# Seven block products instead of eight in two gate pairs and half of the output projection, and the sums of h in a tile of the large pool

## The chip, the core and the metric

The kernel runs on one core of one Trainium2 chip. The metric is the device time of one execution in microseconds (us), as the median of several runs; lower is better.

## What is computed

One layer of a transformer-like trunk over 256 tokens of width 2048, all in float32:

```python
h = rms_norm(x, norm_mix)
proj = h @ w_in                      # 2048 x 11264: q,f,i,g of branch A, q,k,v of branch B, gate logits
gate_a, gate_b = split(sigmoid(gate_logits + b_gate))
y_a = hgrn2_mixer(q_a, f_a, i_a, g_a)        # gated linear recurrence, 8 heads
y_b = chunked_relpos_attention(q_b, k_b, v_b)  # 8 heads
merged = gate_a * (y_a @ w_proj_a) + gate_b * (y_b @ w_proj_b)
x = x + merged @ w_out                        # 2048 x 2048
h = rms_norm(x, norm_ffn)
ff_gate, ff_up = split(h @ w_ffn_in)          # 2048 x 2*5632
out = x + (silu(ff_gate) * ff_up) @ w_ffn_out # 5632 x 2048
```

## The kernel before, in words

**The unit of work.** Every weight matrix is cut into blocks of 512 columns, and each block by rows into chunks (`kc`) of 512 rows, which are four k-tiles of 128. TensorE (PE) multiplies in a 32-bit format that keeps fewer bits than float32, so both operands are split into a high and a low part, and each product is a *triple* of matmuls (high*high, high*low, low*high; lines 162 to 164 and 216 to 218). The 256 tokens are two row blocks `m` of 128. A plain chunk of one block takes 4 k-tiles x 2 row blocks = 8 triples, 24 matmuls of 512 columns.

**Splitting the weights.** `load_weights` (lines 131 to 145) and `halves` (174 to 180) split what a DMA from SP's queue brought (`fetch`, 118): ScalarE (ACT) casts raw weights to the high part `whi` (141, 171), VectorE (DVE) subtracts to get the low part `wlo` (142, 172), two k-tiles at a time. `whi` and `wlo` have four such buffers each, the raw weights eight.

**Seven for eight.** `product_pair` (199 to 268) multiplies two blocks of columns at once. In a chunk whose number is in `forms`, the first two k-tiles x two row blocks x two column blocks are a 2x2x2 block product, made in seven triples instead of eight (`seven`, 223), from sums of blocks: of the weights, `weight_forms` (182) makes four DVE sums `ta`, `tb` (188, tiles of the pool `t6` with two buffers) and splits them; of the activations, `act_forms` (312) makes four sums `sf` (319, or 321 with a gain) and splits them. The other two k-tiles are plain. Seven triples go to eight PSUM banks: four `cb`, which end as results, and four `ub` (products 1, 5, 7, 6), which an epilogue adds on DVE afterwards. There are eight banks in all, four in the pool `mm`, four in `aux`. It is used for half of the blocks of the FFN's first product (`SEVEN_IN`, j = 1, 3, 5, 7, 9) in all four chunks, with the plain k-tiles first in chunk 0, and for the FFN's second product in chunks `SEVEN` = 1, 2, 3, 5, 6, 7, 9.

**Side work.** Generators in `running` (105) emit transposes, attention and recurrence between the triples, one step per `tick()`, every four triples. After FFN block j, `transpose_split` (301) transposes `hn` on PE, splits it into `hT` and, for j in `SEVEN`, makes the sums of h (line 307), which are stored to DRAM (`spill`, 309, a DMA from POOL's queue) and come back later. Those sums are written to a tile of the pool `t6`:

```python
        if j in SEVEN:
            f = t6_p.tile([P, 2, 4, P], F32R, tag="t6", name=nm("sform"))
            spill = kept[j] = dram.tile([P, 2, 4, P], F32, tag=f"kept{j}", name=nm("kept"))
        soon = dict(wait=0, pool=mm) if j + 1 in SEVEN_IN else {}
        start(transpose_split(hn, *hT[j], forms=f, spill=spill, **soon))
```

**The stages in order of time.** Branch A and B projections with recurrence and attention; eight gate products (lines 741 to 753: per nb the blocks of gates a and b); the merge (758 to 768: two half-length products per nb, products with the gates on DVE, their sum on POOL, line 766, then transposes to `mT`); the output projection (775 to 786); the FFN's first product (822 to 839); its second (847 to 877).

**What sets the order.** A planner orders each engine's instructions when the program is built, by priority and by a simulated time, and gives out the buffers of a pool as they come free in that simulation. Weight loading and splitting stand under a priority raised by `PREP_AHEAD` = 500 instructions. Program order of the side work is therefore only a hint; each engine then runs its list in order. The pool `t4` has 33 buffers of 4 KB per partition and holds the activations; `t2` has three of 2 KB.

Of the kernel before, what the change touches and what calls it, by code (L numbers as in the profile page):

```python
# [11 lines left out]
F32R = mybir.dt.float32r  # L12
U32 = mybir.dt.uint32
AF = mybir.ActivationFunctionType
ALU = mybir.AluOpType
AX = mybir.AxisListType

P = 128
T = 256
# [3 lines left out]
NJ = DFF // 512  # L23
# [6 lines left out]
C_NM, C_NF, C_LB, C_OG, C_QG, C_KG = 0, 16, 32, 48, 56, 57  # L30
# [5 lines left out]

SEVEN = (1, 2, 3, 5, 6, 7, 9)

SEVEN_IN = (1, 3, 5, 7, 9)


@with_exitstack
def block_kernel(ctx: ExitStack, tc: tile.TileContext, x, x_t, w_in, w_pa, w_pb, w_out, w_fi, w_fo,
                 params, b_gate, bias, masks, out):
    nc = tc.nc
# [6 lines left out]
    t6_p = ctx.enter_context(tc.tile_pool(name="t6", bufs=2))  # L52
    t2_p = ctx.enter_context(tc.tile_pool(name="t2", bufs=3))
    mm = ctx.enter_context(tc.tile_pool(name="mm", bufs=4, space=bass.MemoryType.PSUM))
    aux = ctx.enter_context(tc.tile_pool(name="aux", bufs=4, space=bass.MemoryType.PSUM))
# [4 lines left out]
    def nm(s):  # L60
        uid[0] += 1
        return f"{s}_{uid[0]}"

    def t4(shape, s, dt=F32):
        return big.tile(shape, dt, tag="t4", name=nm(s))
# [4 lines left out]
    def t2(shape, s):  # L70
        return t2_p.tile(shape, F32, tag="t2", name=nm(s))
# [19 lines left out]
    for _ in range(N_WARM):  # L91
        nc.tensor.matmul(warm_ps[:, 0:256], lhsT=warm[:, 0:P], rhs=warm, start=True,
                         stop=True)

    def rsqrt_mean(dst, ss, n):

# [15 lines left out]
    def start(g):  # L112
        running.append(g)
# [187 lines left out]
    def transpose_split(nat, hi, lo, gain=None, wait=2, pool=aux, forms=None, spill=None):  # L301
        for _ in range(wait):
            yield 1
        for pair in range(2):
            pt = transpose_split_pair(nat, pair, hi, lo, gain, pool)
            if forms is not None and pair == 0:
                act_forms(pt, forms, gain)
                if spill is not None:
                    nc.gpsimd.dma_start(out=spill, in_=forms.bitcast(F32))
            yield 1  # L310
# [30 lines left out]
    par = cpool.tile([P, NPAR], F32, tag="par", name="par")  # L341
    xs = []
    xT = []
    ss_x = cpool.tile([P, 2, 4], F32, tag="ss_x", name="ss_x")
    r1 = cpool.tile([P, 2], F32, tag="r1", name="r1")
# [6 lines left out]
    def rstd_rows(ss, r):  # L352
        tot = t_small([P, 8], "tot")
        nc.vector.tensor_reduce(out=tot[:, 0:2], in_=ss, axis=AX.X, op=ALU.add)
        rsqrt_mean(r, tot[:, 0:2], D)
# [31 lines left out]
    act_x = picker(xT)  # L387
# [335 lines left out]
    for half in range(2):  # L723
        ps = ps_f0 if half == 0 else product(w_in, 2 + half, 4, act_x)
        b, kk, qT = (t4([P, 4, T], s) for s in ("b", "kk", "qT"))
# [12 lines left out]
        start(after(1, attention(half, 0, qT, kT, v, *ybT[half])))  # L738
        start(after(4, attention(half, 1, qT, kT, v, *ybT[half])))

    gates = {}
    for nb in range(4):
        for br in range(2):
            c = 4 * br + nb
            bg = t2([P, 512], "bg")
            nc.sync.dma_start(out=bg, in_=b_gate[c:c + 1, :].to_broadcast([P, 512]))
            ps = product(w_in, 14 + c, 4, act_x)
            gt = t4([P, 2, 512], "gate")
            for m in range(2):
                nc.vector.scalar_tensor_tensor(out=gt[:, m, :], in0=ps[m], scalar=r1[:, m:m + 1],  # L750
                                               in1=bg, op0=ALU.mult, op1=ALU.add)
                nc.scalar.activation(gt[:, m, :], gt[:, m, :], AF.Sigmoid)
            gates[br, nb] = gt


    act_a, act_b = picker(yaT), picker(ybT)
    mT = []
    for nb in range(4):
        ga, gb = gates[0, nb], gates[1, nb]
        ps = product(w_pa, nb, 2, act_a)  # L760
        for m in range(2):
            nc.vector.tensor_tensor(out=ga[:, m, :], in0=ps[m], in1=ga[:, m, :], op=ALU.mult)
        ps = product(w_pb, nb, 2, act_b)
        for m in range(2):
            nc.vector.tensor_tensor(out=gb[:, m, :], in0=ps[m], in1=gb[:, m, :], op=ALU.mult)
            nc.gpsimd.tensor_tensor(out=gb[:, m, :], in0=ga[:, m, :], in1=gb[:, m, :], op=ALU.add)
        mT.append(split_tiles("mT"))
        start(transpose_split(gb, *mT[nb]))


    act_m = picker(mT)
    x2T, x2_kept, fx = [], [], {}
    ss2 = cpool.tile([P, 2, 4], F32, tag="ss2", name="ss2")
    r2 = cpool.tile([P, 2], F32, tag="r2", name="r2")
    for nb in range(4):
        ps = product(w_out, nb, 4, act_m)
        for m in range(2):
            nc.vector.tensor_tensor(out=xs[nb][:, m, :], in0=ps[m], in1=xs[nb][:, m, :],
                                    op=ALU.add)
        x2T.append(split_tiles("x2T"))  # L780
        fx[nb] = t4([P, 2, 4, P], "fx", F32R)
        start(transpose_split(xs[nb], *x2T[nb], gain=par[:, C_NF + 4 * nb:C_NF + 4 * nb + 4],
                              forms=fx[nb]))
        sumsq_block(xs[nb], ss2, nb)
        x2_kept.append(dram.tile([P, 2, 512], F32, tag=f"x2_{nb}", name=nm("x2")))
        nc.gpsimd.dma_start(out=x2_kept[nb], in_=xs[nb])
    rstd_rows(ss2, r2)


    act_x2 = picker(x2T)  # L790
    hT = []
    kept = {}
    def add(out, a, b):
        nc.vector.tensor_tensor(out=out, in0=a, in1=b, op=ALU.add)

    def up_times(hn, m, up):
        nc.vector.scalar_tensor_tensor(out=hn[:, m, :], in0=up, scalar=r2[:, m:m + 1],
                                       in1=hn[:, m, :], op0=ALU.mult, op1=ALU.mult)
# [1 line left out]
    def swiglu_pair(j):  # L800
        hn = t4([P, 2, 512], "hn")
        u = []

        def sums(ub):
            u.extend(t2([P, 512], "u") for _ in range(2))
            nc.scalar.copy(hn[:, 0, :], ub[1])
            add(u[0], ub[6], hn[:, 0, :])
            add(hn[:, 1, :], ub[7], u[0])
            add(u[1], ub[5], hn[:, 1, :])
            add(u[0], ub[5], u[0])  # L810

        cb = product_pair(w_fi, (j, NJ + j), 4, act_x2, fx, aux, mm, sums, plain_first=True,
                          last=True)
        for m in range(2):
            add(hn[:, m, :], cb[m, 0], hn[:, m, :])
            nc.scalar.activation(hn[:, m, :], hn[:, m, :], AF.Silu, scale=r2[:, m:m + 1])
        for m in range(2):
            add(u[m], cb[m, 1], u[m])
            up_times(hn, m, u[m])
        return hn  # L820

    for j in range(NJ):
        if j in SEVEN_IN:
            hn = swiglu_pair(j)
        else:
            ps = product(w_fi, j, 4, act_x2)
            hn = t4([P, 2, 512], "hn")
            for m in range(2):
                nc.scalar.activation(hn[:, m, :], ps[m], AF.Silu, scale=r2[:, m:m + 1])
            ps = product(w_fi, NJ + j, 4, act_x2)  # L830
            for m in range(2):
                up_times(hn, m, ps[m])
        hT.append(split_tiles("hT"))
        f = spill = None
        if j in SEVEN:
            f = t6_p.tile([P, 2, 4, P], F32R, tag="t6", name=nm("sform"))
            spill = kept[j] = dram.tile([P, 2, 4, P], F32, tag=f"kept{j}", name=nm("kept"))
        soon = dict(wait=0, pool=mm) if j + 1 in SEVEN_IN else {}
        start(transpose_split(hn, *hT[j], forms=f, spill=spill, **soon))

    act_h = picker(hT)
    out_v = out.rearrange("(m p) d -> p m d", p=P)
    forms = {}
# [3 lines left out]
    for pair in range(2):  # L847
        nbs = (2 * pair, 2 * pair + 1)
        xs = {nb: t4([P, 2, 512], "x2") for nb in nbs}
        for nb in nbs:  # L850
            nc.gpsimd.dma_start(out=xs[nb], in_=x2_kept[nb])
        x0, x1 = (xs[nb] for nb in nbs)

        def sums(ub):

            u2, u3 = t2([P, 512], "u2"), t2([P, 512], "u3")
            add(x0[:, 0, :], x0[:, 0, :], ub[1])
            nc.scalar.copy(u2, ub[1])
            add(u2, ub[6], u2)
            add(u3, ub[7], u2)  # L860
            add(x1[:, 0, :], x1[:, 0, :], u2)
            add(x0[:, 1, :], x0[:, 1, :], u3)
            add(x1[:, 1, :], x1[:, 1, :], u3)
            for m in range(2):
                add(x1[:, m, :], ub[5], x1[:, m, :])

        pools = (mm, aux) if pair == 0 else (aux, mm)
        cb = product_pair(w_fo, nbs, NJ, act_h, forms, *pools, sums, last=pair == 1)
        for n, nb in enumerate(nbs):
            for m in range(2):  # L870
                pieces = 2 if nb == 3 and m == 1 else 1
                w = 512 // pieces
                for i in range(pieces):
                    sl = slice(i * w, (i + 1) * w)
                    add(xs[nb][:, m, sl], cb[m, n][:, sl], xs[nb][:, m, sl])
                    nc.sync.dma_start(out=out_v[:, m, nb * 512 + i * w:nb * 512 + (i + 1) * w],
                                      in_=xs[nb][:, m, sl])
# [63 lines left out]
```

## Time and profile before

| what | us |
|---|---|
| median of 3 runs | 1447.47 (1447.43 to 1447.57) |
| the profiled execution, its own time | 1449.29 |
| its span, first to last instruction | 1447.5 |
| PE busy | 1431.1 (99%) |
| VectorE busy | 990.4 (68%) |
| ScalarE busy | 749.2 (52%) |
| GpSimd busy | 48.5 (3%) |

The mean granted clock of TensorE is 0.995 of full speed, and the DMA queues moved 287 MB. A matmul's row shows the start and a modelled end; matmuls overlap, so the distance of their starts is what one costs, not its duration. Some matmul rows are missing from the trace. Idle time stands in brackets at the end of a row, with what ended it.

### The profile page before, as it was taken

The numbers are of one execution on the slowest core, as the hardware profiler recorded it, in microseconds if no ns is written. First come the engines' busy times: TensorE is split into PE (matmuls) and PEld (weight loads), VectorE is DVE, ScalarE is ACT, GpSimd is POOL, SyncE is SP. The second block draws the span as 40 slices with busy tenths as digits, with TensorE's granted clock in tenths as the row PEclk, the third lists the DMA queues.
The fourth block names the chain that finished last, engine by engine and source line by source line (L and its number), as shares of the span: only waits on it lengthen the run. The fifth ranks groups of instructions, "written<-read, shape, count | busy, mean of one in ns | idle before, by whom it ended". The sixth has DMA issues, their size and how long they took to land.

```text
span 1447.5 us, 17485 instructions
## 1 busy us (share of the span) xinstructions
PE 1431.1 (99%) x6484; PEld 1185.8 (82%) x6484; DVE 990.4 (68%) x1225; ACT 749.2 (52%) x966; POOL 48.5 (3%) x59
## 2 busy tenths in 40 slices
PE   8999999999999999999999999999999999999998
PEld 7888888888888888888888877888778888888887
DVE  6768869564654555556658768687686876777876
ACT  6756655555544444445555535455354554454553
POOL 0100100100000000100000000000000001000000
PEclk9999999999999999999999999999999999999999
DMA  9654454456556665556655646656466578666662
GB/s 356 235 196 154 137 198 148 168 172 207 181 198 203 203 192 191 189 183 218 204 194 177 227 150 213 208 178 228 147 216 207 178 236 314 230 200 224 203 190 85
DMA packets 81526, 287.32 MB, mean 198 GB/s; under 512 B 9120, under 2 KB 9376, under 8 KB 81440
## 3 DMA queue, kind: packets, MB, share of 16 engines
q1 hardware_dynamic: 78272, 274.66, 57.1%
q0 software_dynamic: 3168, 11.54, 2.1%
q8 instruction: 51, 0.84, 0.2%
q14 instruction: 35, 0.29, 0.1%
HBM read 278.30 MB, written 7.86 MB: 198 GB/s over the span
## 4 chain that ended last, share of the span: by engine, by line
PE 88%; issue 9%; DMA 1%; DVE 1%; ACT 0%; SPq 0%; POOL 0%; DVEq 0%; ACTq 0%; POOLq 0%
PE mm L162 19%; PE mm L164 19%; PE mm L163 19%; PE mp L216 9%; PE mp L217 9%; PE mp L218 9%; PE bank L279 2%; PE bank L537 1%; DMA xt<-in_x_t 1%; DMA kept<-sform 0%; PE bank L567 0%; PE bank L613 0%; PE bank L664 0%; ACT whi L171 0%; DVE tb L188 0%
## 5 line engine op out<-in xcount | busy, mean ns | idle before, releaser
L142 DVE TENSOR_TENSOR wlo<-raw,whi 128x1024 fp32r<-128x1024 f32 (+1 forms) x340 | 411.5, 1215 | 283.8 <-ACT whi L141 283.4
L141 ACT CAST whi<-raw 128x1024 fp32r<-128x1024 f32 (+1 forms) x340 | 352.9, 1042 | 384.6 <-PE mm L164 332.1
L162 PE MATMUL mm<-whi,xTh 128*128 128x512 f32 x704 | 276.9, 397 | 2.5 <-ACT whi L141 2.5
L164 PE MATMUL mm<-whi,xTl 128*128 128x512 f32 x704 | 274.9, 390 | 0.0
L163 PE MATMUL mm<-wlo,xTh 128*128 128x512 f32 x704 | 274.8, 390 | 0.0
L172 DVE TENSOR_TENSOR wlo<-raw,whi 128x1024 fp32r<-128x1024 f32 (+1 forms) x168 | 183.2, 1112 | 37.9 <-ACT whi L171 37.2
L171 ACT CAST whi<-raw 128x1024 fp32r<-128x1024 f32 (+1 forms) x168 | 157.0, 965 | 98.8 <-PE mp L218 53.6
L162 PEld LDWEIGHTS mm<-whi,xTh 128*128 128x128 f32 x704 | 132.1, 188 | 29.4 <-ACT whi L141 3.6
L164 PEld LDWEIGHTS mm<-whi,xTl 128*128 128x128 f32 x704 | 132.2, 188 | 27.6
L163 PEld LDWEIGHTS mm<-wlo,xTh 128*128 128x128 f32 x704 | 132.3, 188 | 26.9 <-DVE wlo L142 0.9
L162 PE MATMUL mm<-whi,x2Th 128*128 128x512 f32 x384 | 150.0, 391 | 0.0
L164 PE MATMUL mm<-whi,x2Tl 128*128 128x512 f32 x384 | 149.5, 389 | 0.0
L163 PE MATMUL mm<-wlo,x2Th 128*128 128x512 f32 x384 | 149.4, 389 | 0.0
L217 PE MATMUL mp<-wlo,hTh 128*128 128x512 f32 x282 | 109.7, 389 | 0.0
L218 PE MATMUL mp<-whi,hTl 128*128 128x512 f32 x282 | 109.6, 389 | 0.0
L216 PE MATMUL mp<-whi,hTh 128*128 128x512 f32 x282 | 99.7, 390 | 0.0
L218 PE MATMUL mp<-whi,x2Tl 128*128 128x512 f32 x220 | 87.5, 398 | 0.0
L217 PE MATMUL mp<-wlo,x2Th 128*128 128x512 f32 x220 | 87.4, 397 | 0.0
L164 PEld LDWEIGHTS mm<-whi,x2Tl 128*128 128x128 f32 x384 | 72.1, 188 | 15.0
L163 PEld LDWEIGHTS mm<-wlo,x2Th 128*128 128x128 f32 x384 | 72.1, 188 | 14.8
L162 PEld LDWEIGHTS mm<-whi,x2Th 128*128 128x128 f32 x384 | 72.1, 188 | 14.8
L216 PE MATMUL mp<-whi,x2Th 128*128 128x512 f32 x220 | 79.7, 405 | 0.0
(221 smaller groups left out, 1898.5 us busy)
## 6 DMA issues: line engine op xcount, KB each, us to landing
raw<-in_w_fi SPq DMA_DIRECT2D x176, 512.0 KB, 4.6
raw<-in_w_in SPq DMA_DIRECT2D x172, 512.0 KB, 4.4
raw<-in_w_fo SPq DMA_DIRECT2D x88, 512.0 KB, 5.0
raw<-in_w_out SPq DMA_DIRECT2D x32, 512.0 KB, 3.6
raw<-in_w_pa SPq DMA_DIRECT2D x16, 512.0 KB, 4.5
raw<-in_w_pb SPq DMA_DIRECT2D x16, 512.0 KB, 4.6
x<-x POOLq DMA_DIRECT2D x8, 512.0 KB, 4.6
kept<-sform POOLq DMA_DIRECT2D x7, 512.0 KB, 4.6
```

The costliest lines, as they stand in the source:

```text
L141: nc.scalar.copy(hi[:, sl, :], src[:, sl, :])
L142: nc.vector.tensor_tensor(out=lo[:, sl, :], in0=src[:, sl, :], in1=hi[:, sl, :].bitcast(F32), op=ALU.subtract)
L162: nc.tensor.matmul(ps[m], lhsT=ah, rhs=wh, start=kc == 0 and k4 == 0, stop=False)
L163: nc.tensor.matmul(ps[m], lhsT=ah, rhs=wl, start=False, stop=False)
L164: nc.tensor.matmul(ps[m], lhsT=al, rhs=wh, start=False, stop=kc == n_chunks - 1 and k4 == 3)
L171: nc.scalar.copy(hi, src)
L172: nc.vector.tensor_tensor(out=lo, in0=src, in1=hi.bitcast(F32), op=ALU.subtract)
L216: nc.tensor.matmul(ps, lhsT=ah, rhs=wh, start=first, stop=False)
L217: nc.tensor.matmul(ps, lhsT=ah, rhs=wl, start=False, stop=False)
L218: nc.tensor.matmul(ps, lhsT=al, rhs=wh, start=False, stop=final)
L279: nc.tensor.transpose(out=pt[:, j, m * P:(m + 1) * P], in_=nat[:, m, c:c + P], identity=ident)
L537: nc.tensor.matmul(pl[:, j, :], lhsT=ek[:, g // 2, (g % 2) * P:(g % 2 + 1) * P], rhs=eq[:, g, :], start=True, stop=True)
```

## The change

Three things, and helpers that move:

- The gates of nb = 1 and nb = 3 (`SEVEN_GATE`): the blocks of gate a and gate b become one `product_pair` with sums in all four chunks, `cb` in `aux` and `ub` in `mm`. The sums of x that it needs (`fq`) are made by a new generator `x_forms`, started ahead of the gates: it loads two of four k-tiles of each chunk of x transposed once more (POOL's queue), and makes the sums with the gain.
- The output projection's column blocks 0 and 1 (`SEVEN_OUT`) become one `product_pair`. The sums of the merged activations (`fm`) are made in the transposes of the merge; those of nb = 3 come one tick earlier than before and in the pool `mm`. Residual add, transposes and sums of squares of both blocks follow together.
- The sums of h (`sform`) are written to a `t4` tile instead of a `t6` tile.

```diff
+SEVEN_GATE = (1, 3)
+SEVEN_OUT = (0,)
...
-    gates = {}
+    def four_sums(ub, e00, e10, e01, e11):
+        nc.scalar.copy(e00, ub[1])
+        add(e01, ub[6], e00)
+        add(e10, ub[7], e01)
+        add(e11, ub[5], e10)
+        add(e01, ub[5], e01)
+
+    def x_forms():
+        for c in range(4):
+            xt = t4([P, 2, T], "xt2")
+            nc.gpsimd.dma_start(out=xt, in_=x_t[c, :, 0:2, :])
+            fq[c] = t4([P, 2, 4, P], "fq", F32R)
+            yield 1
+            yield 1
+            act_forms(xt, fq[c], par[:, C_NM + 4 * c:C_NM + 4 * c + 4])
+
+    gates, fq = {}, {}
+    start(x_forms())
     for nb in range(4):
+        bgs, gts = [], []
         for br in range(2):
             c = 4 * br + nb
...
+            if nb in SEVEN_GATE:
+                continue
             ps = product(w_in, 14 + c, 4, act_x)
...
+        if nb in SEVEN_GATE:
+            def sums(ub):
+                for br in range(2):
+                    gates[br, nb] = t4([P, 2, 512], "gate")
+                four_sums(ub, *(gates[br, nb][:, m, :] for br in range(2) for m in range(2)))
+
+            cb = product_pair(w_in, (14 + nb, 18 + nb), 4, act_x, fq, aux, mm, sums,
+                              plain_first=True, last=True)
+            for br in range(2):
+                gt = gates[br, nb]
+                for m in range(2):
+                    add(gt[:, m, :], cb[m, br], gt[:, m, :])
+                    nc.vector.scalar_tensor_tensor(out=gt[:, m, :], in0=gt[:, m, :],
+                                                   scalar=r1[:, m:m + 1], in1=bgs[br],
+                                                   op0=ALU.mult, op1=ALU.add)
+                    nc.scalar.activation(gt[:, m, :], gt[:, m, :], AF.Sigmoid)
...
-        start(transpose_split(gb, *mT[nb]))
+        fm[nb] = t4([P, 2, 4, P], "fm", F32R)
+        soon = dict(wait=1, pool=mm) if nb == 3 else {}
+        start(transpose_split(gb, *mT[nb], forms=fm[nb], **soon))
...
+    def residual_sums(x0, x1):      # the second FFN product's epilogue, moved here
+        ...
+    for pair in range(2):
+        nbs = (2 * pair, 2 * pair + 1)
+        if pair in SEVEN_OUT:
+            cb = product_pair(w_out, nbs, 4, act_m, fm, aux, mm,
+                              residual_sums(xs[nbs[0]], xs[nbs[1]]), plain_first=True, last=True)
+            for n, nb in enumerate(nbs):
+                norm_block(nb, [cb[m, n] for m in range(2)])
+        else:
+            for nb in nbs:
+                norm_block(nb, product(w_out, nb, 4, act_m))
...
-            f = t6_p.tile([P, 2, 4, P], F32R, tag="t6", name=nm("sform"))
+            f = t4([P, 2, 4, P], "sform", F32R)
```

`norm_block` is the body of the old loop over the output blocks (residual add, transposes, sum of squares, store of x). `residual_sums` has one ACT copy and eight DVE adds.

## Rows read from the trace of the kernel before

**Rows 1.** The page: busy time of each engine; the chain that ended last.

```profile
PE 1431.1 (99%) x6484; PEld 1185.8 (82%) x6484; DVE 990.4 (68%) x1225; ACT 749.2 (52%) x966; POOL 48.5 (3%) x59
...
PE 88%; issue 9%; DMA 1%; DVE 1%; ACT 0%; SPq 0%; POOL 0%; DVEq 0%; ACTq 0%; POOLq 0%
```

**Rows 2.** Who PE waited for: us in total, times, longest.

```profile
PE mp L216 <- ACT whi L171: 7.8, 4, 3.0
...
PE mp L217 <- DVE wlo L172: 1.1, 2, 0.5
```

**Rows 3.** PE in order of time in a plain gate product: start, duration, line.

```profile
437.65 0.39 PE L163 MATMUL mm<-wlo,xTh 128*128 128x512 f32 x1
...
446.49 0.39 PE L163 MATMUL mm<-wlo,xTh 128*128 128x512 f32 x1
```

**Rows 4.** Stretches: length, PE, PEld, DVE, ACT, POOL busy (count), granted clock, DMA, GB/s.

```profile
819.85:914.14 94.29, 89.94 (x391) 73.12 (x390) 68.03 (x83) 46.05 (x54) 1.11 (x2) 0.96 0.58 190
...
914.14:1000.41 86.27, 86.27 (x391) 71.33 (x390) 66.19 (x78) 45.45 (x52) 0.53 (x1) 1.00 0.60 201
...
1000.41:1094.89 94.48, 90.02 (x392) 73.23 (x390) 68.03 (x83) 46.08 (x54) 1.07 (x2) 0.96 0.56 190
...
1094.89:1181.15 86.26, 86.26 (x392) 71.34 (x389) 66.12 (x78) 45.47 (x52) 0.53 (x1) 1.00 0.60 201
...
870.00:880.00 10.00, 9.13 (x27) 7.10 (x28) 7.59 (x10) 5.33 (x6) 0.00 (x0) 0.66 0.75 245
```

**Rows 5.** PE in order of time, j = 3, where it idled.

```profile
865.54 0.73 PE L216 MATMUL mp<-whi,fx 128*128 128x512 f32 x2 [0.96 <-ACT whi L171]
...
866.80 0.50 PE L217 MATMUL mp<-wlo,fx 128*128 128x512 f32 x1 [0.53 <-DVE wlo L172]
...
870.87 0.79 PE L216 MATMUL mp<-whi,fx 128*128 128x512 f32 x1 [2.86 <-ACT whi L171]
```

**Rows 6.** DVE in order of time at the start of j = 3.

```profile
860.42 0.28 DVE L319 TENSOR_TENSOR sf<-bank,sf 128x128 f32<-128x128 f32 x1
...
863.08 0.68 DVE L188 TENSOR_TENSOR ta<-raw,raw 128x512 f32<-128x512 f32 x1
...
868.24 0.69 DVE L188 TENSOR_TENSOR tb<-ta,raw 128x512 f32<-128x512 f32 x1 [1.49 <-DMA kept<-sform]
```

**Rows 7.** DVE, then PE, in order of time at j = 1.

```profile
778.34 1.23 DVE L172 TENSOR_TENSOR wlo<-tb,whi 128x1024 fp32r<-128x1024 f32 x1
...
780.18 0.39 PE L217 MATMUL mp<-wlo,fx 128*128 128x512 f32 x1
```

**Rows 8.** Groups by line and shape: total us, mean ns of one | idle before.

```profile
L319 DVE TENSOR_TENSOR sf<-bank,sf 128x128 f32<-128x128 f32 x28 | 7.6, 286 | 0.4
...
L172 DVE TENSOR_TENSOR sform<-sf,sform 128x512 fp32r<-128x512 f32 x7 | 4.8, 685 | 0.0
...
L321 DVE SCALAR_TENSOR_TENSOR sf<-bank,par,sf 128x128 f32<-128x128 f32 x16 | 5.2, 344 | 0.1
...
L188 DVE TENSOR_TENSOR ta<-raw,raw 128x512 f32<-128x512 f32 x34 | 23.4, 690 | 15.2 <-DMA raw<-in_w_fi 9.1 <-DMA raw<-in_w_fo 5.6
...
L172 DVE TENSOR_TENSOR wlo<-ta,whi 128x1024 fp32r<-128x1024 f32 x34 | 41.6, 1224 | 45.7 <-ACT whi L171 45.7
...
L794 DVE TENSOR_TENSOR u<-mp,u 128x512 f32<-128x512 f32 x19 | 12.5, 678 | 0.0
```

**Rows 9.** The same view: two gate products, the merge, two output products.

```profile
391.00:434.50 43.50, 43.50 (x200) 36.25 (x199) 21.62 (x20) 20.55 (x24) 0.00 (x0) 1.00 0.60 195
...
547.00:637.50 90.50, 90.50 (x412) 74.85 (x411) 54.41 (x55) 36.63 (x38) 14.14 (x8) 1.00 0.57 189
...
683.20:728.70 45.50, 45.50 (x210) 37.61 (x209) 29.12 (x40) 24.44 (x36) 1.79 (x3) 1.00 0.62 208
```

**Rows 10.** POOL and DVE in order of time at the merge's end.

```profile
629.98 3.54 POOL L766 TENSOR_TENSOR gate<-gate,gate 128x512 f32<-128x512 f32 x2 [19.22 <-DVE gate L765]
...
630.73 1.63 DVE L142 TENSOR_TENSOR wlo<-raw,whi 128x1024 fp32r<-128x1024 f32 x1 [0.30 <-ACT whi L141]
```

More of the change, by code (lines that the diff above doesn't have):

```diff
@@ L93, in block_kernel, with add @@
                          stop=True)
+    def add(out, a, b):
+        nc.vector.tensor_tensor(out=out, in0=a, in1=b, op=ALU.add)
     def rsqrt_mean(dst, ss, n):
@@ L742, in block_kernel @@
+    gates, fq = {}, {}
+    start(x_forms())
     for nb in range(4):
+        bgs, gts = [], []
         for br in range(2):
             c = 4 * br + nb
-            bg = t2([P, 512], "bg")
-            nc.sync.dma_start(out=bg, in_=b_gate[c:c + 1, :].to_broadcast([P, 512]))
+            bgs.append(t2([P, 512], "bg"))
+            nc.sync.dma_start(out=bgs[br], in_=b_gate[c:c + 1, :].to_broadcast([P, 512]))
+            if nb in SEVEN_GATE:
+                continue
             ps = product(w_in, 14 + c, 4, act_x)
-            gt = t4([P, 2, 512], "gate")
+            gt = gates[br, nb] = t4([P, 2, 512], "gate")
@@ L749, in block_kernel @@
             for m in range(2):
                 nc.vector.scalar_tensor_tensor(out=gt[:, m, :], in0=ps[m], scalar=r1[:, m:m + 1],
-                                               in1=bg, op0=ALU.mult, op1=ALU.add)
+                                               in1=bgs[br], op0=ALU.mult, op1=ALU.add)
                 nc.scalar.activation(gt[:, m, :], gt[:, m, :], AF.Sigmoid)
-            gates[br, nb] = gt
+        if nb in SEVEN_GATE:
[13 more added lines that the diff above has]
+                    nc.scalar.activation(gt[:, m, :], gt[:, m, :], AF.Sigmoid)
@@ L756, in block_kernel @@
     act_a, act_b = picker(yaT), picker(ybT)
-    mT = []
+    mT, fm = [], {}
     for nb in range(4):
@@ L774, in block_kernel, with sums, norm_block @@
     r2 = cpool.tile([P, 2], F32, tag="r2", name="r2")
-    for nb in range(4):
-        ps = product(w_out, nb, 4, act_m)
+    def residual_sums(x0, x1):
+        def sums(ub):
+            u2, u3 = t2([P, 512], "u2"), t2([P, 512], "u3")
+            add(x0[:, 0, :], x0[:, 0, :], ub[1])
+            nc.scalar.copy(u2, ub[1])
+            add(u2, ub[6], u2)
+            add(u3, ub[7], u2)
+            add(x1[:, 0, :], x1[:, 0, :], u2)
+            add(x0[:, 1, :], x0[:, 1, :], u3)
+            add(x1[:, 1, :], x1[:, 1, :], u3)
+            for m in range(2):
+                add(x1[:, m, :], ub[5], x1[:, m, :])
+        return sums
+    def norm_block(nb, ps):
         for m in range(2):
-            nc.vector.tensor_tensor(out=xs[nb][:, m, :], in0=ps[m], in1=xs[nb][:, m, :],
-                                    op=ALU.add)
+            add(xs[nb][:, m, :], ps[m], xs[nb][:, m, :])
         x2T.append(split_tiles("x2T"))
@@ L792, in block_kernel @@
     kept = {}
-    def add(out, a, b):
-        nc.vector.tensor_tensor(out=out, in0=a, in1=b, op=ALU.add)
     def up_times(hn, m, up):
@@ L805, in sums @@
             u.extend(t2([P, 512], "u") for _ in range(2))
[L806 to L810, printed above, removed]
+            four_sums(ub, hn[:, 0, :], hn[:, 1, :], *u)
         cb = product_pair(w_fi, (j, NJ + j), 4, act_x2, fx, aux, mm, sums, plain_first=True,
@@ L852, in block_kernel @@
         x0, x1 = (xs[nb] for nb in nbs)
[L854 to L865, printed above, removed]
         pools = (mm, aux) if pair == 0 else (aux, mm)
-        cb = product_pair(w_fo, nbs, NJ, act_h, forms, *pools, sums, last=pair == 1)
+        cb = product_pair(w_fo, nbs, NJ, act_h, forms, *pools,
+                          residual_sums(x0, x1), last=pair == 1)
         for n, nb in enumerate(nbs):
```

## The prediction

> **What bounds the kernel now.** First the page: PE is busy for 1431.1 of 1447.5 us, and the chain that ended last runs through PE for 88% of the span, with 9% of "issue" between PE's own instructions [rows 1]. So time goes only where PE gets fewer instructions, or where it stops waiting. What a matmul costs is read from starts: from one low-part matmul at 437.65 to the one at 446.49 there are 13 triples, 39 matmuls, so 8.84 / 39 = 0.2267 us each, at a granted clock of 1.00; the 0.39 in the rows overlap [rows 3].
>
> Then who PE waited for: in the pairs, 7.8 us for ACT's casts of `whi` in four waits and 1.1 us for `wlo` [rows 2]. The table of stretches finds the place. Two FFN blocks, a plain one and a pair, take 86.27 and 86.26 us where the pair is j = 5 or 9, and 94.29 and 94.48 us where it is j = 3 or 7 [rows 4]: 8.02 and 8.22 us more for the same matmuls. PE's order of time at j = 3 shows idle stretches of 0.96, 0.53 and 2.86 us, 4.35 together [rows 5]; just behind them the granted clock over ten us is 0.66, so part of that time ran at 1.2 GHz instead of 2.4 [rows 4]. The rest of the 8 us, some 3.7, is that. DVE's order of time shows the cause: the forms of h (line 319) are made from 860.42 on, `ta` of the next chunk only starts at 863.08, and `tb` waits until 868.24 for the DMA that stores `sform` [rows 6]. `sform`, `ta` and `tb` share the two buffers of `t6`; `sform` keeps one until it is stored. j = 3 and 7 are the pairs behind a block that leaves forms (2 and 6); ahead of j = 1, 5 and 9 none are made.
>
> **The change part by part.**
>
> *Fewer matmuls.* Each chunk of a pair with sums has 15 triples instead of 16. Two gate pairs x 4 chunks and one output pair x 4 chunks are 12 triples, 36 matmuls: 36 x 0.2267 = 8.2 us off PE [rows 3]. No transposes are added. This is exact as long as PE stays the bound.
>
> *sform in t4.* The 8.02 + 8.22 = 16.2 us at j = 3 and 7 have the `t6` wait as their last cause [rows 4, 6]. With `sform` elsewhere, `ta` and `tb` can be made as at j = 1. Does `t4` have room? At j = 7 there live 8 tiles of x2T, 4 of fx, 14 of hT, two hn and `sform`, 29 of 33; in j = 8 it is 31. What is late next is DVE itself: the forms are still made there, 4 x 0.286 + 0.685 = 1.83 us [rows 8], between the transposes and the weights of chunk 1. At j = 1, where they are absent, `wlo` from `tb` for chunk 1 ends at 778.34 + 1.23 = 779.57 and PE takes it at 780.18 [rows 7]: 0.6 us in hand. So about 1.83 - 0.6 = 1.2 us of lateness comes back, each time. Bounds: 0, if the planner puts the forms where DVE idles, and the whole 8.1 us if something else than the tile holds DVE up. I take 1.2, since the `t6` wait is in the row and its cause is removed.
>
> *Weight forms in three more pairs.* A chunk of a pair with sums asks of DVE four sums at 0.69, one subtraction of 512 at about 0.685 (as long as the one on `sform`) and five of 1024 at 1.224: 2.76 + 0.69 + 6.12 = 9.6 us [rows 8], against 45 x 0.2267 = 10.2 us of PE. Plain it is 4 x 1.22 = 4.9. So DVE goes from under half to 94% of PE's time, and nothing hides it if it falls behind: each us late is a us of PE. The nearest rows are the pairs j = 5 and 9, four such chunks in a row, with the transposes of `hn` on top, in a stretch in which PE has no idle time [rows 4]. The gate pairs have no transposes beside them, so less DVE work than those: I take 0, between 0 and the 8.1 us of j = 3; a gain below 0 is excluded, since PE shows no idle time in the gates now [rows 9]. The output pair begins like j = 3 with forms, those of the merge's nb = 3, but free of a `t6` tile: I take 1.2 again, between 0 and 8.1.
>
> *Sums of x.* Per chunk four DVE operations at 0.344 and one of 0.685, 2.06 us, 8.2 in all [rows 8], and on ACT two instructions. They fall in the first two gate products, of which DVE uses 21.6 us in 43.5 [rows 9]; needed from the first pair on. Cost 0; if they slip into that pair, up to 8.1. The four loads of x go on POOL's queue, behind which only POOL's small work waits, and add 1 MB to 287; each has over 20 us to land.
>
> *Sums of merged.* For nb = 0 to 2, 1.83 us each within a merge of which DVE uses 54 in 90 us [rows 9]: 0.
>
> *Epilogues.* A gate pair adds eight DVE additions at 0.68 and a copy on ACT, the output pair eight additions, 5.4 us each [rows 8]. The `ub` banks are emptied during the last 24 matmuls (5.4 us) of the pair, the rest during the plain product behind it, where DVE uses half of the time. In the output projection, where DVE uses 29.1 of 45.5 us [rows 9], both blocks' transposes now fall on one product: weights 8 x 1.23, two blocks' splits and forms about 8, additions 2.7, 20.5 of 21.8 us. Hidden, with the weights first by priority. If it isn't, PE waits for the excess; I keep 1 us for that in the range.
>
> *The sum left by POOL.* The output pair starts while POOL still adds the last merged block, two additions in 3.54 us; a DVE subtraction beside them took 1.63 instead of 1.23 us [rows 10], 0.4 us in a stretch where DVE has idle time: 0. The Trainium skill (SBUF — State Buffer, Who interferes with whom) has a stricter rule: a DVE instruction with two SBUF inputs and a GpSimd instruction that reads SBUF share a read port by an exclusive lock, and the loser blocks for the whole instruction. By it the pair could start up to 3.5 us later on DVE, and the sum would be smaller by up to that; the row bears out that they collide, but not a block of a whole POOL instruction.
>
> Sum: -8.2 - 16.2 + 3 x 1.2 = -20.8 us. The span of 1447.5 would be 1426.7; the execution's own 1449.29 lies 1.8 above its span and the median of the runs, 1447.47, equals the span, so I apply the difference to the median: 1426.7 us.
>
> **Rivals.**
>
> *All of it hidden.* The planner finds room for the forms in all three places: 1447.5 - 24.4 = 1423.1. For it: DVE idles somewhere in every pair. Against: at j = 1 it does so before the transposes or late, not between.
>
> *Short waits that cost the clock.* At j = 3, idle stretches of 4.35 us were followed by 3.7 us lost at 1.2 GHz [rows 4, 5]. If the three places with forms keep a wait of 1.2 us and it is enough for the fall, each costs 1.2 + 3.7 = 4.9: 1423.1 + 14.7 = 1437.8; one such place gives 1428. Against: the stretch's clock is 1.00 wherever PE had no long wait. The Trainium skill (TensorE: Matmul & The Clock Gate, HAM oscillation) states that an engine that idles between bursts drops to the half rate and pays for it at each burst; by it the price would be paid at every place with a wait long enough, which here the one place j = 3 and its twin j = 7 show.
>
> *The tile is not the cause.* If the forms' work on DVE and not `sform`'s buffer holds j = 3 and 7, they keep their 8.1 us each and the output pair, built the same way, gains one: 1447.5 - 8.2 + 8.1 = 1447.4, no change. For it: the first two idle stretches, 0.96 + 0.53 us, come from `ta` behind the forms. Against: the longest follows the wait for the DMA.
>
> *Slower.* DVE at 94% in every pair is overdrawn by any side work, and the planner puts the sums of x, which stand low in its order, into the first gate pair, and the epilogue of a pair ahead of weights. Then all three new pairs stall like j = 3, while j = 3 and 7 stay: 1447.5 - 8.2 + 3 x 8.1 = 1463.6; with one gate pair spared, 1455.5. It decides where side work in a pair's first chunks exceeds the 0.6 us in hand and holds a buffer until it is done. Against: the transposes beside j = 1, 5 and 9, 1.4 us of DVE, leave PE without idle time.
>
> **How the numbers follow.** Forecast (1424 to 1430): 0.42. All hidden: 0.23. Waits with the clock, 1430 to 1439: 0.20. The tile not the cause, or gains eaten elsewhere, 1439 to 1450: 0.07. Slower: 0.08. The range 1422 to 1438 leaves out about 0.17; its low end has 1 us for planner's luck. What a measurement of this kernel can tell from no change is about 0.2%, 2.9 us: faster than 1444.6 in all of the first three, 0.85, and half of a small rest, 0.86; same 0.06; slower 0.08.
>
> **What would show it.** 36 matmuls fewer on PE, in lines 216 to 218's place of 162 to 164. Two FFN blocks of about 86.3 to 87.5 us for all pairs, and no wait of `tb` for a store. The first two gate products and the pair together 84.3 us instead of 87. An idle stretch of about a us on PE early in j = 3, j = 7 and the output pair, with the clock at 1.00. Wrong it is if the j = 3 stretch still takes 94 us, if a gate pair shows idle PE time, or if the clock falls anywhere between the gates and the FFN's end.

## The result

The changed kernel takes 1427.88 us (median of 4 runs, 1427.22 to 1428.46), against 1447.52 before: 19.6 us less, a ratio of 0.9864 with the 95% interval 0.9847 to 0.9881. Forecast were 1426.7 and a range of 1422 to 1438. The profiled execution took 1427.22 us, 1.8 above its span of 1425.4.

The page of the changed kernel, the two lines that answer to [rows 1]:

```profile
PE 1417.6 (99%) x6448; PEld 1174.4 (82%) x6448; DVE 1063.6 (75%) x1361; ACT 774.2 (54%) x1009; POOL 50.1 (4%) x63
...
PE 98%; DVE 1%; ACT 0%; DMA 0%; issue 0%; SPq 0%; DVEq 0%; ACTq 0%
```

PE has 36 matmuls fewer (6484 to 6448), DVE is busy for 73 us more and still has room on the average. What PE waited for, to compare with [rows 2] (us in total, times, longest):

```profile
PE mm L168 <- ACT whi L147: 1.3, 1, 1.3
PE mp L222 <- ACT whi L177: 1.1, 2, 0.5
```

In the pairs, 8.9 us of waits became 1.1; the other row lies in the first microseconds of the kernel. The stretches of [rows 4], at the same points of PE's work, then the two gate pairs, and the output projection (the pair, then two plain blocks):

```profile
811.74:899.15 87.41, 86.87 (x391) 71.17 (x390) 67.53 (x83) 46.14 (x54) 1.11 (x2) 1.00 0.62 205
899.15:985.42 86.27, 86.27 (x391) 71.34 (x390) 66.12 (x78) 45.44 (x52) 0.53 (x1) 1.00 0.60 201
985.42:1072.77 87.35, 86.80 (x391) 71.20 (x390) 67.53 (x83) 46.11 (x54) 1.06 (x2) 1.00 0.61 205
1072.77:1159.04 86.27, 86.27 (x391) 71.34 (x390) 66.20 (x78) 45.46 (x52) 0.53 (x1) 1.00 0.62 201
407.44:448.49 41.05, 41.05 (x183) 33.91 (x181) 35.71 (x41) 24.14 (x27) 0.00 (x0) 1.00 0.60 196
491.78:532.62 40.84, 40.84 (x181) 33.72 (x180) 35.48 (x41) 24.15 (x27) 0.00 (x0) 1.00 0.57 192
622.63:666.24 43.61, 43.39 (x190) 34.25 (x189) 39.70 (x50) 24.95 (x29) 3.00 (x2) 1.00 0.52 176
666.24:712.35 46.11, 46.11 (x217) 38.22 (x215) 35.75 (x54) 27.94 (x46) 1.64 (x3) 1.00 0.69 234
```

The stretches with j = 3 and 7 fell from 94.29 and 94.48 us to 87.41 and 87.35, those with j = 5 and 9 stay at 86.27. The granted clock is 1.00 in each of these rows. A gate pair takes 40.8 to 41.1 us, 180 x 0.2267 = 40.8, and DVE is busy for 35.5 of them. PE's order of time at j = 3 has one idle stretch in place of the three of [rows 5], and DVE's has no wait for the store of `sform` any more (compare [rows 6]); first PE, then DVE, then ACT:

```profile
857.13 0.50 PE L222 MATMUL mp<-whi,x2Th 128*128 128x512 f32 x1 [0.54 <-ACT whi L177]
```

```profile
848.39 0.69 DVE L194 TENSOR_TENSOR ta<-raw,raw 128x512 f32<-128x512 f32 x1
...
852.30 0.28 DVE L325 TENSOR_TENSOR sf<-bank,sf 128x128 f32<-128x128 f32 x1
852.50 0.68 DVE L194 TENSOR_TENSOR tb<-ta,raw 128x512 f32<-128x512 f32 x1
...
855.03 0.28 DVE L325 TENSOR_TENSOR sf<-bank,sf 128x128 f32<-128x128 f32 x1
855.24 0.68 DVE L194 TENSOR_TENSOR tb<-raw,tb 128x512 f32<-128x512 f32 x1
...
860.64 0.68 DVE L178 TENSOR_TENSOR sform<-sf,sform 128x512 fp32r<-128x512 f32 x1
```

```profile
856.03 1.05 ACT L177 CAST whi<-tb 128x1024 fp32r<-128x1024 f32 x1 [0.68 <-DVE tb L194]
```

The sums of h (`sf`) now stand between the weights' sums (`tb`), not all ahead of them, and `ta` of the next chunk is made at 848.39, ahead of the first of them, where before it came at 863.08, behind the last. So the tile held DVE up in two ways, by the planner's order and by the wait for the store; moving it changes both, and no run takes them apart. What is left, PE's idle 0.54 us, ends with ACT's cast of `tb`, and that cast waited for DVE.

By stage, profile against profile: up to the end of the gates 6.6 us less, merge 0.2, output projection 1.3 (91.0 to 89.7), first FFN product 14.0 (492.1 to 478.1), second 0.0 (235.0 both): 22.1. The medians differ by 19.6 only. The profile of before was on its high side: the profiled execution took 1449.29 us, against a median of 1447.52, and the kernel before took 1445.84 to 1448.49 us in 16 runs beside the first experiments and up to 1449.93 beside the last. Of the 6.6 us, 1.1 lie in the first 30 us of the two executions, which the change doesn't touch.

### The profile page after: what moved, and what is told of

It reads as the page before. It is cut to its first block, busy times and chain, and to the rows that moved or that the text cites. A ratio compares the mean times of both kernels' runs of the same rounds, so it can differ in the third digit from the quotient of the medians.

```text
span 1425.4 us, 17596 instructions
## 1 busy us (share of the span) xinstructions
PE 1417.6 (99%) x6448; PEld 1174.4 (82%) x6448; DVE 1063.6 (75%) x1361; ACT 774.2 (54%) x1009; POOL 50.1 (4%) x63
## 4 chain that ended last, share of the span: by engine, by line
PE 98%; DVE 1%; ACT 0%; DMA 0%; issue 0%; SPq 0%; DVEq 0%; ACTq 0%
PE mm L169 18%; PE mm L168 18%; PE mm L170 18%; PE mp L223 13%; PE mp L224 13%; PE mp L222 13%; PE bank L285 2%; PE bank L543 1%; DVE wlo L178 1%; ACT whi L177 0%; PE bank L573 0%; DMA raw<-in_w_in 0%; PE bank L619 0%; PE bank L670 0%; PE bank L698 0%; DVE tb L194 0%
## 5 line engine op out<-in xcount | busy, mean ns | idle before, releaser
L148 DVE TENSOR_TENSOR wlo<-raw,whi 128x1024 fp32r<-128x1024 f32 (+1 forms) x292 | 351.9, 1212 | 175.6 <-ACT whi L147 173.4
L147 ACT CAST whi<-raw 128x1024 fp32r<-128x1024 f32 (+1 forms) x292 | 301.9, 1040 | 292.7 <-PE mm L170 219.8
L178 DVE TENSOR_TENSOR wlo<-raw,whi 128x1024 fp32r<-128x1024 f32 x216 | 235.0, 1110 | 51.9 <-ACT whi L177 50.8
L177 ACT CAST whi<-raw 128x1024 fp32r<-128x1024 f32 x216 | 201.2, 960 | 121.8 <-PE mp L224 59.6
L168 PE MATMUL mm<-whi,xTh 128*128 128x512 f32 x576 | 226.6, 398 | 1.3 <-ACT whi L147 1.3
L169 PE MATMUL mm<-wlo,xTh 128*128 128x512 f32 x576 | 225.2, 391 | 0.0
L170 PE MATMUL mm<-whi,xTl 128*128 128x512 f32 x576 | 225.1, 391 | 0.0
L169 PEld LDWEIGHTS mm<-wlo,xTh 128*128 128x128 f32 x576 | 108.3, 188 | 21.8 <-DVE wlo L148 1.0
L177 ACT CAST whi<-ta 128x1024 fp32r<-128x1024 f32 x46 | 48.3, 1050 | 89.9 <-PE mp L224 87.4
L178 DVE TENSOR_TENSOR wlo<-ta,whi 128x1024 fp32r<-128x1024 f32 x46 | 56.2, 1223 | 48.3 <-ACT whi L177 48.3
```

Of the source, the lines that this page charges most:

```text
L147: nc.scalar.copy(hi[:, sl, :], src[:, sl, :])
L148: nc.vector.tensor_tensor(out=lo[:, sl, :], in0=src[:, sl, :], in1=hi[:, sl, :].bitcast(F32), op=ALU.subtract)
L168: nc.tensor.matmul(ps[m], lhsT=ah, rhs=wh, start=kc == 0 and k4 == 0, stop=False)
L169: nc.tensor.matmul(ps[m], lhsT=ah, rhs=wl, start=False, stop=False)
L170: nc.tensor.matmul(ps[m], lhsT=al, rhs=wh, start=False, stop=kc == n_chunks - 1 and k4 == 3)
L177: nc.scalar.copy(hi, src)
```

## The experiments

**One part at a time.** Only the sums of h in t4:

```diff
-SEVEN_GATE = (1, 3)
-SEVEN_OUT = (0,)
+SEVEN_GATE = ()
+SEVEN_OUT = ()
-    start(x_forms())
-        start(transpose_split(gb, *mT[nb], forms=fm[nb], **soon))
+        start(transpose_split(gb, *mT[nb]))
```

> The kernel before with only the sums of h moved from t6 to t4; gates and output projection all plain. Theory (the stalls of j = 3 and 7 are the wait for the t6 tile): the two FFN stretches with j = 3 and j = 7 fall from 94.3 and 94.5 us to about 87.4, as in the changed kernel, 14 us off the span, so 1433.5; if the timed runs of the kernel before lost less in these stalls than its profiled one, up to 1435.5. Rival (the forms' work on VectorE is the cause, and the planner's new order in the whole program healed it): stretches stay at 94, 1447.

Measured: 1435.09 us (1434.86 to 1435.31), ratio 0.9917 (0.9904 to 0.9931), 12.3 below the kernel before beside it. The stretch with j = 3 (that with j = 7 takes 87.39):

```profile
806.89:894.29 87.40, 86.86 (x389) 71.24 (x388) 67.53 (x83) 46.11 (x53) 1.11 (x2) 1.00 0.63 208
```

The tile alone brings both stretches to what they are in the changed kernel. The opposite edit, the changed kernel with the sums of h back in t6:

```diff
-            f = t4([P, 2, 4, P], "sform", F32R)
+            f = t6_p.tile([P, 2, 4, P], F32R, tag="t6", name=nm("sform"))
```

> The changed kernel with only the sums of h put back in t6. Theory: j = 3 and 7 stall again with 4.35 us of idle time and the lower clock behind it, 87.4 becomes 94.4 in both stretches, 1427.9 + 12 to 14 = 1440 to 1442; tb waits for the store of sform. Rival (other order, not the tile): stays near 1428.

Measured: 1441.52 us (1439.04 to 1441.94), ratio 0.9963 (0.9949 to 0.9976). The stalls are back; the stretches and ten us of j = 3, then PE and DVE there:

```profile
798.73:891.86 93.13, 88.61 (x390) 72.26 (x388) 68.12 (x83) 46.10 (x53) 1.11 (x2) 0.98 0.59 192
978.12:1071.77 93.65, 88.97 (x389) 72.31 (x388) 68.11 (x83) 46.04 (x53) 1.06 (x2) 0.98 0.59 192
860.00:870.00 10.00, 7.29 (x25) 5.78 (x26) 9.01 (x11) 5.35 (x6) 0.00 (x0) 0.83 0.64 208
```

```profile
857.23 0.73 PE L222 MATMUL mp<-whi,fx 128*128 128x512 f32 x2 [0.96 <-ACT whi L177]
858.49 0.50 PE L223 MATMUL mp<-wlo,fx 128*128 128x512 f32 x1 [0.53 <-DVE wlo L178]
862.71 0.79 PE L222 MATMUL mp<-whi,fx 128*128 128x512 f32 x1 [3.03 <-ACT whi L177]
```

```profile
860.08 0.69 DVE L194 TENSOR_TENSOR tb<-ta,raw 128x512 f32<-128x512 f32 x1 [1.65 <-DMA kept<-sform]
```

`ta` comes behind all the forms again, at 854.76, and `tb` waits for the store. Idle time is 4.52 us, against 4.35 before, but the loss is 5.7 us in the one stretch and 6.3 in the other (93.13 and 93.65 less 87.4), where the profile of before had 6.9 and 7.1. How long the lower clock lasts behind nearly the same wait differs from one execution to the next: a granted clock of 0.83 over ten us is some 3.4 us at the lower of the two levels here, and the 0.66 of [rows 4] some 6.8 us (estimates from these two rows). Whether this is why the kernel before scatters by several us isn't shown: of the 16 runs beside the first experiments those at a mean clock of 0.995 took 1447.6 to 1448.49 us and those at 0.997 took 1445.84 and 1446.87, but the 11 runs beside the last ones don't order that way.

Only the gate pairs, and only the output pair (sums of h in t6 in both):

```diff
 # gates only                      # output only
-SEVEN_OUT = (0,)                  -SEVEN_GATE = (1, 3)
+SEVEN_OUT = ()                    +SEVEN_GATE = ()
```

> The kernel before with only the two gate pairs by seven products (sums of x included); sums of h in t6, output projection plain. Theory (PE alone sets the pace there): 24 matmuls x 0.2267 = 5.4 us less, 1442.0, with no idle time of PE in the gates. Rival (the sums of x or VectorE at 94% cost time): each gate pair above 38.6 us, 1443 to 1447.

> The kernel before with only the first two output blocks by seven products. Theory: 12 matmuls x 0.2267 = 2.7 us less, and 1.2 to 1.4 us back as short waits in the pair's second chunk, because the forms of the last merged block stand on VectorE ahead of its weights: 1446.2. Rival (all hidden): 1444.8. Rival (waits that bring the lower clock): 1448 or more.

Measured: gates 1442.62 us (1442.01 to 1444.19), ratio 0.9971 (0.9959 to 0.9982); output 1446.44 us (1445.3 to 1448.15), ratio 0.9997 (0.9988 to 1.0006), which by itself can't be told from nothing. Their traces can: the first gate pair of the one (the second takes 40.84), then the output pair of the other.

```profile
407.97:449.03 41.06, 41.06 (x183) 33.94 (x181) 35.71 (x41) 24.15 (x27) 0.00 (x0) 1.00 0.58 194
```

```profile
628.60:672.22 43.62, 43.41 (x191) 34.27 (x190) 39.70 (x50) 24.94 (x29) 3.00 (x2) 1.00 0.54 180
```

PE never idles in the gate pairs. (The 38.6 us in the expectation is a slip: 180 matmuls take 40.8 us.) All three pairs are as long as in the changed kernel, to 0.01 us, so in these stretches the parts don't act on each other. By medians they add up to 12.3 + 4.7 + 0.9 = 17.9 us, 1.7 short of the 19.6 of all three, which the scatter of the runs allows.

**What is left at j = 3, j = 7 and in the output pair.** Without the forms at j = 3 and 7:

```diff
-SEVEN = (1, 2, 3, 5, 6, 7, 9)
+SEVEN = (1, 3, 5, 7, 9)
```

> The changed kernel without sums of h in chunks 2 and 6 (SEVEN = 1, 3, 5, 7, 9): the second FFN product has 12 matmuls more, +2.7 us, and j = 3 and 7 have no forms beside them. Theory (the forms' four sums on VectorE are what is left there): both stretches fall from 87.4 to 86.3, -2.2 us; together +0.5, 1428.4. Rival (what is left has another cause): stretches stay at 87.4, 1430.6.

Measured: 1428.87 us (1427.14 to 1429.68). The changed kernel wasn't run beside this experiment and the next three; the kernel before took 1448.06 us there, 0.5 more than in the first comparison, so that the stretches decide and not the medians. The stretch with j = 3 (that with j = 7 takes 86.26), then the second FFN product (235.0 in the changed kernel):

```profile
800.01:886.28 86.27, 86.27 (x389) 71.34 (x388) 66.13 (x78) 45.47 (x51) 0.58 (x1) 1.00 0.60 202
1189.25:1426.96 237.71, 233.71 (x1035) 193.23 (x1033) 160.46 (x172) 107.07 (x109) 0.55 (x1) 1.00 0.56 185
```

No forms, no wait; and 12 matmuls cost 2.7 us where PE is the bound. The forms of the last merged block left out in the same way (the output pair's last chunk plain):

```diff
-        fm[nb] = t4([P, 2, 4, P], "fm", F32R)
+        if nb < 3:
+            fm[nb] = t4([P, 2, 4, P], "fm", F32R)
...
-        start(transpose_split(gb, *mT[nb], forms=fm[nb], **soon))
+        start(transpose_split(gb, *mT[nb], forms=fm.get(nb), **soon))
```

> The changed kernel without the sums of the last merged block: the output pair's last chunk is plain, 3 matmuls more, +0.7 us. Theory: the 1.4 us of short waits in the pair's second chunk go, 1427.9 - 0.7 = 1427.2. Rival (the waits come from the sum left by GpSimd or the earlier transposes): they stay, 1428.6.

Measured: 1427.54 us (1426.69 to 1428.91), not to be told from the changed kernel by time. The whole output projection:

```profile
623.22:712.50 89.28, 89.18 (x408) 73.42 (x407) 70.10 (x92) 50.52 (x71) 4.63 (x5) 1.00 0.61 206
```

That is 0.4 us less than the 89.72 of the changed kernel with 0.7 us more of matmuls, so 1.1 of the 1.4 us went. More work for DVE at j = 3 and 7:

```diff
+        for _ in range(1 + again):   # again = 5 after j = 2 and 6
             op(s[:, 0, :], a22, 1, s[:, 2, :], ALU.add)
```

> The changed kernel with the first sum of the forms of h made six times instead of once after j = 2 and 6, 5 x 0.286 = 1.43 us more on VectorE at each place, same output. Theory (VectorE is late by what stands ahead of the weights, one to one, and short waits don't cost the clock): each stretch 87.4 + 1.4 = 88.8, 1427.9 + 2.9 = 1430.8, clock 1.00. Rival (a wait of 2.5 us costs the clock as 4.35 us did): up to 3.7 us more each, 1438. Rival (0.6 us and more in hand somewhere): less than 1 us each.

Measured: 1430.65 us (1429.62 to 1432.84). The two stretches, and PE's two waits at j = 3:

```profile
800.50:889.20 88.70, 87.50 (x389) 71.00 (x388) 68.69 (x88) 46.23 (x53) 1.11 (x2) 1.00 0.60 202
975.46:1064.12 88.66, 87.48 (x389) 71.01 (x388) 68.76 (x88) 46.23 (x53) 1.06 (x2) 1.00 0.61 204
```

```profile
858.50 0.50 PE L222 MATMUL mp<-whi,x2Th 128*128 128x512 f32 x1 [0.35 <-ACT whi L177]
...
862.55 0.50 PE L223 MATMUL mp<-wlo,x2Th 128*128 128x512 f32 x1 [0.75 <-DVE wlo L178]
```

The five sums are 1.43 us by their rows, but a row is longer than the distance to the next start (0.28 and 0.20 us at 852.30 above); DVE is busy for 1.16 and 1.23 us more, and PE lost 1.3 us more at each place, with the clock at 1.00. So DVE is the bound in a pair's first chunks, and its lateness passes on about one to one. This speaks against the rival of short waits that cost the clock: 2.4 us lost in two waits and in the slower starts behind them did not lower it, 4.35 us of idle time in three waits did. The Trainium skill (TensorE: Matmul & The Clock Gate, HAM oscillation) has the half rate follow idle gaps between bursts; the trace agrees for the long wait and shows none for the short ones.

The four sums on GpSimd instead, from a copy in SBUF:

```diff
+        if on_pool:                  # after j = 2 and 6, and the last merged block
+            sb = t2([P, 2, T], "sb")
+            nc.scalar.copy(sb, pt)
+            pt = sb
...
+                nc.gpsimd.tensor_tensor(out=out, in0=x, in1=y, op=o)
```

> The changed kernel with the four sums of the forms on GpSimd for h after j = 2 and 6 and for the last merged block, from a copy that ScalarE makes of the transposed block. Theory: VectorE loses 1.14 us at each of the three places, the 1.1 + 1.1 + 1.4 us of waits go, 1427.9 - 3.6 = 1424.3. Rival (GpSimd's reads slow VectorE's subtractions as beside the merge's sum, 0.4 us per pair of sums, or block them for whole instructions): 1426 to 1430.

Measured: 1428.06 us (1426.53 to 1428.89), a miss: no gain that the medians show. The whole output projection, where 0.8 of the 1.4 us went (89.72 in the changed kernel), and the j = 3 stretch, where nothing did; then POOL's order of time at j = 3, then DVE's:

```profile
624.21:713.16 88.95, 88.77 (x406) 72.69 (x404) 74.80 (x99) 52.92 (x75) 7.75 (x9) 1.00 0.62 207
799.74:887.09 87.35, 86.86 (x389) 71.19 (x388) 67.34 (x79) 46.41 (x53) 4.27 (x6) 1.00 0.62 207
```

```profile
852.40 0.94 POOL L329 TENSOR_TENSOR sf<-sb 128x128 f32<-128x128 f32 x2 [34.24 <-ACT sb L323]
853.31 2.30 POOL L329 TENSOR_TENSOR sf<-sb,sf 128x128 f32<-128x128 f32 x2
```

```profile
853.12 0.77 DVE L194 TENSOR_TENSOR tb<-ta,raw 128x512 f32<-128x512 f32 x1
853.82 2.34 DVE L178 TENSOR_TENSOR wlo<-raw,whi 128x1024 fp32r<-128x1024 f32 x2
...
857.82 0.68 DVE L178 TENSOR_TENSOR sform<-sf,sform 128x512 fp32r<-128x512 f32 x1
858.42 1.21 DVE L178 TENSOR_TENSOR wlo<-tb,whi 128x1024 fp32r<-128x1024 f32 x1
```

At j = 3 the rows show two things that make up for the 1.14 us. The pair of subtractions at 853.82 took 2.34 us; the same pair took 1.81 in the run without forms, with GpSimd idle, and the sum ahead of it 0.77 instead of 0.68: 0.6 us of collision. And the planner, with the forms ready sooner, put their low-part subtraction (0.68) ahead of the weights'. The Trainium skill (SBUF — State Buffer, Who interferes with whom) says that DVE instructions with two SBUF inputs contend with GpSimd's reads for a shared port; the trace agrees that they collide, on both sides (POOL's second two sums took 2.30 us, the first two 0.94; the quickest of either kind in this run took 0.46 and 0.45 each), with DVE losing 0.6 us to 3.2 us of POOL's work, not all of it.

**A version that beats both.** Just before the transposes of a pair, DVE idles 2.29 us, because ACT waits until PE has done with a `whi` buffer; the rows of the changed kernel at j = 3, DVE, then ACT:

```profile
847.13 1.23 DVE L178 TENSOR_TENSOR wlo<-ta,whi 128x1024 fp32r<-128x1024 f32 x1 [2.29 <-ACT whi L177]
```

```profile
846.05 1.05 ACT L177 CAST whi<-ta 128x1024 fp32r<-128x1024 f32 x1 [2.10 <-PE mp L224]
```

With five buffers they could work ahead. Two versions pay for them from other pools:

```diff
 # six raw buffers                        # 31 tiles
-wraw bufs=8, whi bufs=4, wlo bufs=4      -big bufs=33, whi bufs=4, wlo bufs=4
+wraw bufs=6, whi bufs=5, wlo bufs=5      +big bufs=31, whi bufs=5, wlo bufs=5
```

> The changed kernel with five buffers each for the high and low parts of the weights instead of four, paid for by six raw buffers instead of eight. Theory (VectorE is late in a pair's first chunks because it idles 2.3 us just before the transposes for want of a whi buffer): with one buffer more it works ahead, the waits of 1.1, 1.1 and 1.4 us go, 1427.9 - 3.6 = 1424.3. Rival (the raw weights come late with six buffers): waits for the DMA of raw on PE, 1428 or more.

> The same five buffers, paid for by 31 instead of 33 tiles in t4. Theory: as above, 1424.3, if 31 tiles do. Rival (t4 is full around the gates and at j = 9, where 32 or 33 tiles are alive by count): PE waits for a tile there, several us, above 1430.

> The changed kernel once more beside them on this chip: 1427.2 to 1428.5 as before; both theories say the same.

Measured on one chip: the changed kernel 1428.51 us (1427.84 to 1428.8), six raw buffers 1441.15 (1438.08 to 1442.79), 31 tiles 1424.47 (1423.15 to 1425.06), with ratios to before of 0.9864 (0.9852 to 0.9877), 0.9951 (0.9937 to 0.9964) and 0.9835 (0.9823 to 0.9848). With six raw buffers the rival came true in kind: PE waited for the low parts, and DVE for the DMAs of raw weights (us in total, times, longest):

```profile
PE mp L223 <- DVE wlo L178: 13.1, 10, 2.4
...
DVE ta L194 <- DMA raw<-in_w_fo: 43.3, 13, 5.2
```

With 31 tiles the stretch with j = 3 (that with j = 7 takes 86.19), then the whole output projection, then the row of DVE at j = 3 that idled for 2.29 us:

```profile
799.28:885.44 86.16, 86.16 (x389) 71.40 (x388) 67.45 (x83) 45.96 (x53) 1.11 (x2) 1.00 0.62 206
624.26:712.81 88.55, 88.44 (x405) 72.88 (x404) 75.88 (x103) 53.20 (x75) 5.18 (x5) 1.00 0.61 208
```

```profile
844.76 1.23 DVE L178 TENSOR_TENSOR wlo<-ta,whi 128x1024 fp32r<-128x1024 f32 x1 [0.33 <-ACT whi L177]
```

1.2 + 1.2 + 1.2 us (89.72 to 88.55) are gone, as expected: 4.0 us below the changed kernel, 24.6 below the one before. The forms still cost DVE the same (67.45 and 67.46 us busy, 67.53 in the changed kernel); it only makes its weights earlier. That 31 tiles would do was not clear: by my count 32 to 33 are alive at the last gates and at j = 9; no wait for a tile shows on PE, and why the count did no harm isn't shown.

## Why the prediction was right

- *Fewer matmuls, 8.2 us:* right. 36 fewer; the gate pairs run at 0.2267 us per matmul without idle time, alone as well (gates only: 4.7 us by medians of 5.4 forecast).
- *sform in t4, 16.2 us less what comes back:* right in place and cause: moving the tile alone brings 12.3 us, moving it back costs 13.6, and the wait of `tb` for the store goes and comes with it. The 16.2 is the high side, taken from one execution in which the clock stayed low for long; by medians the tile is worth 12.3 to 13.6 us net instead of 13.8. The wait for the store is one part of the cause: the other, `ta` behind all the forms, is in the prediction's account of DVE, but it has no term of its own.
- *1.2 us back at three places:* measured 1.14 and 1.08 (87.41 and 87.35 less 86.27) and 1.4 in the output pair (89.72 less 91.01 - 2.72). The size is right, and partly by luck: both readings behind it, 1.83 us of work and 0.6 in hand, are too large. DVE's rows overlap, so the forms keep it busy for 1.4 us, not 1.83 (67.53 in the stretch against 66.13 without forms), and the last of them, `sform`'s subtraction at 860.64, starts behind PE's wait at 857.13. And the 0.6 was read at `wlo`, while PE's idle time ended with a cast of `tb` to `whi`. At j = 1 before, that cast ends at 777.26 + 1.05 = 778.31 and the next weight load of `whi` starts at 778.38, 0.1 us later (ACT, then PE's weight loads):

```profile
777.26 1.05 ACT L171 CAST whi<-tb 128x1024 fp32r<-128x1024 f32 x1 [1.22 <-DVE tb L188]
```

```profile
778.38 0.19 PEld L216 LDWEIGHTS mp<-whi,fx 128*128 128x128 f32 x1
```

In DVE's busy time 1.4 us of forms cost 1.1, and 2.6 cost 2.4, so 0.1 to 0.3 us are in hand.

- *Weight forms, sums of x, sums of merged, epilogues, 0:* right, with more room than forecast: DVE is busy for 87% of a gate pair (35.48 of 40.84 us) instead of 94%, again because its rows overlap. PE has no idle time from the gates to the end of the merge, nor in the two plain output blocks, where DVE is busy for 35.8 of 46.1 us.
- *The sum left by POOL, 0:* right where the collision can be seen: at 623.59 a subtraction of 512 took 1.47 us in place of 0.68 beside POOL's sum, and DVE then idled for 1.58 us, waiting for `whi`. Why the output pair's 1.4 us is 0.3 above j = 3's stays open.
- *Rivals.* "The tile is not the cause" falls by the two edits of the tile; "short waits that cost the clock" by the added work; "slower" by the gate pairs; "all hidden" was wrong for this kernel and nearly true with five buffers.
- *The sum.* Profile against profile 22.1 us went, 21.0 without the first 30 us, where 20.8 were forecast. The medians differ by 19.6, because the profile of before stood 1.8 us above the median of its runs and that of the changed kernel 0.7 below its own. The forecast set a difference of profiles against a median; that it still came within 1.2 us is chance within the scatter.
- *A reading that was wrong.* The 9% of "issue" in the chain of before don't lie between PE's own instructions. They are two pieces, in which the chain runs back through the store of `sform` at j = 7 to POOL's queue, which issued it; in the changed kernel the chain has none:

```profile
919.58 85.85 issue
...
1005.99 39.91 issue
1045.91 2.89 DMA kept<-sform
```

That is 125.8 us of POOL's idle time and no time that the change could win. The prediction drew nothing from it; read rightly, it is the first sign of the store.

## What to carry to other kernels

A tile that waits for a DMA to leave should not share a pool with tiles that the critical engine needs next: compare the stretches in which it does with those in which it doesn't, and price the stall with the clock that falls behind it. Where an engine is near its limit only at the start of a stage, a buffer more, so that it can work ahead, was worth more here (4.0 us) than taking work off it (no gain by the medians). Before a difference between two profiles is set against a median, see where each profile stands among the runs of its own kernel.

## What the runs showed of the hardware

Nearly the same wait, 4.35 to 4.5 us, cost 5.7 to 7.1 us beyond what is left without it, by how long TensorE stayed at the lower of its two clocks behind it; two waits of 1.1 us together left the granted clock at 1.00. They cost more than their idle time all the same, because the starts behind a wait stand further apart: 0.34 us at 857.13, where 0.23 is the pace. VectorE's rows overlap: a sum of 0.28 us takes 0.20 of a busy VectorE. GpSimd's small sums were no free help: at j = 3, 3.2 us of them cost VectorE 0.6 us.
